# A chunked RWKV-7 recurrence inside a decoder block: the state stacked over the values, 128-row products, batched inverses and a group norm by tokens

## The chip, the cores and the metric

The kernel runs on one core of a Trainium2 chip and is measured in microseconds of device time. Before the change the median of three runs is 2665.36 us (2660.77 to 2671.39). The names of the engines in this text are those of the profile: PE is TensorE (PEld its weight loads), DVE is VectorE, ACT is ScalarE, POOL is GpSimd, SP is SyncE, which issues every DMA of this kernel.

## What is computed

One decoder block on 2048 tokens of width 1024. The input is normed and modulated and multiplied by a combined projection `z = h @ w_in`. Part of `z` feeds a pooling mixer, the rest a RWKV-7 mixer of 8 heads of 64 channels, whose state `S` (64x64 a head) runs through all tokens:

```
def _rwkv7_step(S, inp):
    r, w, k, v, a_vec, b_vec = inp
    sa = jnp.einsum('bhij,bhj->bhi', S, a_vec)
    S = S * w[:, :, None, :] + sa[..., None] * b_vec[:, :, None, :] + v[..., None] * k[:, :, None, :]
    y = jnp.einsum('bhij,bhj->bhi', S, r)
    return S, y
...
    mu = jnp.mean(y, axis=-1, keepdims=True)
    var = jnp.mean(jnp.square(y - mu), axis=-1, keepdims=True)
    yn = ((y - mu) * lax.rsqrt(var + GN_EPS)).reshape(B, T, RWKV_C) * lnx_w + lnx_b
    bonus = jnp.sum(rh * kh * r_k.astype(f32).reshape(N_HEAD, HEAD_N), axis=-1, keepdims=True) * vh
    out = (yn + bonus.reshape(B, T, RWKV_C)) * g
```

Both mixers go through one output projection, the result is added to `x`, and a gated feed-forward layer and a last norm follow.

## The kernel before

The tokens are cut into four batches (`b`) of 512, each batch into 8 chunks (`c`) of 64. There are three stages.

- **Projections.** For each batch `project` makes 18 products of 24 matmuls each (tile `z`, 512 columns). DVE, ACT and POOL make decays, keys and bonuses of them. For every chunk and head the 128x128 Gram products (`gr`, L576) are masked into `gm` and stored in DRAM (`dGM`), beside the decayed queries (`dAR`), keys (`dBH`) and values (`dV`). The 32x32 diagonal blocks are gathered in `N`. `invert` turns them into inverses `W` with 31 steps of a multiply (L284) and an add (L290). For batch 0 that is done here on DVE, for the others later.
- **Chunks.** 32 chunks run one after the other through the state. `chunk` loads its tiles (`cg`, `car`, `cbh`, `cv`), completes the inverse of its 64x64 blocks out of the 32x32 ones (`pq`, L666 and L670, with a copy by ACT behind each), transposes values and keys on PE (`trv`, `trb`), and then walks a chain. `px` is what the Gram block and the state give (L689 from the chunk's own values, L691 from the state `Sb`); ACT copies it to `xx`; `pu` (L699) applies the inverse; ACT copies it into `uv`; `pn` (L704) is the update of the state; two adds by DVE (L707) make the next `Sb`. Beside the chain stands the output `py` (L710 from the state, L713 from `uv`). `Sb` holds two heads block-diagonally, so L691 and L710 take two heads in one matmul. `diagonals(b + 1)` prepares the next batch beside the chunks of this one: it loads `N`, inverts it on POOL and transposes on DVE (L641, L646). After each half of a batch `mixer_norm` makes the group norm with channels in partitions, by products with summing matrices (`pc`, `pv`, `pr`). `out_proj` puts units of 12 projection matmuls of 512 columns (`po`) between the chunks, by a fixed plan.
- **Feed-forward.** Four batches of `gu` and `dn` products of 512 columns.

All products of the chunk stage except `po`, `pc`, `pv` and `pr` are in float32, and each of them stands in the trace as two matmuls (x16 for 8 heads). The order of instructions on every engine is fixed when the program is built: a scheduler that works with its own estimate of times places them, and `issue_after` and `high_priority` bend it. A tile with fewer buffers than users makes the next user wait.

Of the kernel before, what the change touches and what calls it, by code (L numbers as in the profile page):

```python
# [6 lines left out]
F32 = mybir.dt.float32  # L7
F32R = mybir.dt.float32r
AF = mybir.ActivationFunctionType
ALU = mybir.AluOpType  # L10
PSUM = bass.MemoryType.PSUM
# [7 lines left out]
CH = 64  # L19
# [43 lines left out]
def build(tc, io):  # L63
# [39 lines left out]
    dN = [dram.tile([128, 32, 32], F32, name=f"dN{b}") for b in range(NB)]  # L103
    dV = dram.tile([128, 4, 64 + T], F32, name="dV")
# [297 lines left out]
    for b in range(NB):  # L402
# [210 lines left out]
    sp = p1y.tile([128, TB // 2], F32R, name="sp", bufs=1)  # L613
    zero_rows(sp)
    Sb = [p1y.tile([128, 4, 128], F32, name=f"Sb{i}", bufs=1) for i in range(2)]
    G.memset(Sb[0], 0.0)
    G.memset(Sb[1], 0.0)

    for tag, shape, bufs in (("N1", [128, 32, 32], 1), ("W", [128, 32, 32], 1), ("itmp", [128, 256], 1), ("m11", [32, 4, NC, 2, 32], 2)):
        for _ in range(bufs):  # L620
            pe1.tile(shape, F32, tag=tag, name=tag, bufs=bufs)
    MT = pe1.tile([128, 4, NC, 2, 64], F32, name="MT", bufs=1)
    for i in range(2):
        G.memset(MT[64 * i + 32 : 64 * i + 64].rearrange("p a c h t -> p (a c h) t")[:, :, 0:32], 0.0)

    def diagonals(b):
# [3 lines left out]
        W = invert(pe1, N, G) if b else N  # L630
        yield
        o = 64 * (b % 2)
        mu = MT.rearrange("p a c h t -> p (a c h) t")
        m11 = inv[b] = pe1.tile([32, 4, NC, 2, 32], F32, tag="m11", name="m11", bufs=2)
        mm = m11.rearrange("p a c h t -> p (a c h) t")
        for g in range(2):
            us = slice(32 * g, 32 * g + 32)
            for bi in range(2):
# [3 lines left out]
                    mu[o + 32 * bi : o + 32 * bi + 32, us, r].rearrange("p u c -> p c u"),  # L642
# [4 lines left out]
            yield  # L647

    def chunk(b, c, m11, yh, yl):
        o = 64 * (b % 2)  # L650
        mt, lo, hi = MT[o : o + 64], slice(o, o + 32), slice(o + 32, o + 64)
        cc = b * NC + c
        sb, sn = Sb[cc % 2], Sb[(cc + 1) % 2]
        g = p1.tile([128, 8, 128], F32, tag="cg", name="cg", bufs=3)
        Q.dma_start(g, dGM[b][c].rearrange("p x a t -> p (x a) t"))
        a = p1.tile([128, 4, 128], F32, tag="car", name="car")
        Q.dma_start(a, dAR[b][c])
# [4 lines left out]

        qs = p1.tile([128, 8, 32], F32, tag="qs", name="qs")
        ps = ps1.tile([128, 8, 32], F32, tag="gr", name="pq", bufs=1)
        for h in range(8):
            P.matmul(ps[hi, h, :], g[0:32, h, 32:64], m11[:, h // 2, c, h % 2, :], start=True, stop=True)  # L666
# [334 lines left out]
```

## Time and profile before

| | |
|---|---|
| median of the runs | 2665.36 us |
| the profiled execution, its own time | 2662.77 us |
| its span, first to last instruction | 2661.0 us |
| mean granted TensorE clock | 0.976 |
| PE busy | 2531.2 us (95%), 13912 matmuls |
| DVE busy | 1317.1 us (49%) |
| ACT busy | 966.4 us (36%) |
| POOL busy | 457.5 us (17%) |
| DMA | 445.98 MB, mean 168 GB/s |
| chain that ended last | PE 79%, DVE 7%, DMA 6%, ACT 3% |

The busy time of PE counts a matmul from its start to its modelled end, and neighbours overlap. How long a block of matmuls occupies the engine is therefore read from the start of the block to the start of the next one. [...]

### The profile page before, as it was taken

The numbers are of one execution on the slowest core, as the hardware profiler recorded it, in microseconds if no ns is written. First come the engines' busy times: TensorE is split into PE (matmuls) and PEld (weight loads), VectorE is DVE, ScalarE is ACT, GpSimd is POOL, SyncE is SP. The second block draws the span as 40 slices with busy tenths as digits, with TensorE's granted clock in tenths as the row PEclk, the third lists the DMA queues.
The fourth block names the chain that finished last, engine by engine and source line by source line (L and its number), as shares of the span: only waits on it lengthen the run. The fifth ranks groups of instructions, "written<-read, shape, count | busy, mean of one in ns | idle before, by whom it ended". The sixth has DMA issues, their size and how long they took to land.

```text
span 2661.0 us, 35438 instructions
## 1 busy us (share of the span) xinstructions
PE 2531.2 (95%) x13912; PEld 2051.9 (77%) x13912; DVE 1317.1 (49%) x1695; ACT 966.4 (36%) x1490; POOL 457.5 (17%) x516
## 2 busy tenths in 40 slices
PE   5899899997999999799999999999999999999998
PEld 4677677775788878678888888888878888788886
DVE  6668674757567555546334243343343442443322
ACT  3555253443443424423233242332333332333222
POOL 4424333115565300100000020000110000000000
PEclk9899999997999899899999999999999999999998
DMA  8697676876677767655334333234332333333233
GB/s 289 223 314 236 221 268 207 282 258 227 202 246 262 223 218 211 198 185 175 96 101 129 110 127 101 96 95 141 105 127 95 97 104 110 128 101 95 93 111 97
DMA packets 229463, 445.98 MB, mean 168 GB/s; under 512 B 19248, under 2 KB 101424, under 8 KB 229296
## 3 DMA queue, kind: packets, MB, share of 16 engines
q1 hardware_dynamic: 229296, 443.72, 51.2%
q8 instruction: 109, 1.79, 0.3%
q14 instruction: 58, 0.48, 0.1%
HBM read 347.04 MB, written 96.60 MB: 167 GB/s over the span
## 4 chain that ended last, share of the span: by engine, by line
PE 79%; DVE 7%; DMA 6%; ACT 3%; issue 2%; POOL 2%; SPq 0%; DVEq 0%; ACTq 0%; POOLq 0%
PE gu L171 11%; PE gu L170 11%; PE gu L169 11%; PE dn L169 6%; PE dn L170 6%; PE dn L171 6%; PE z L169 3%; PE z L170 3%; PE z L171 3%; PE po L169 2%; PE po L171 1%; PE po L170 1%; DMA wraw<-w_out 1%; PE px L689 1%; PE pu L699 1%
## 5 line engine op out<-in xcount | busy, mean ns | idle before, releaser
L125 DVE TENSOR_TENSOR wlo<-wraw,whi 128x1024 fp32r<-128x1024 f32 (+2 forms) x354 | 400.4, 1131 | 902.7 <-PE gu L170 423.2
L124 ACT CAST whi<-wraw 128x1024 fp32r<-128x1024 f32 (+2 forms) x354 | 337.2, 952 | 780.4 <-DMA wraw<-w_gu 368.9
L169 PE MATMUL gu<-h2h,whi 128*128 128x512 f32 x1408 | 549.3, 390 | 4.5 <-ACT whi L124 4.5
L171 PE MATMUL gu<-h2h,wlo 128*128 128x512 f32 x1408 | 549.7, 390 | 3.6 <-DVE wlo L125 3.6
L170 PE MATMUL gu<-h2l,whi 128*128 128x512 f32 x1408 | 549.0, 390 | 0.0
L241 POOL TENSOR_TENSOR acc<-acc,sq 128x512 f32<-128x512 f32 x76 | 106.2, 1397 | 1451.4 <-ACT sq L237 1150.6
L171 PEld LDWEIGHTS gu<-h2h,wlo 128*128 128x128 f32 x1408 | 264.7, 188 | 61.7 <-DVE wlo L125 7.0
L169 PEld LDWEIGHTS gu<-h2h,whi 128*128 128x128 f32 x1408 | 264.7, 188 | 61.3 <-ACT whi L124 6.4
L170 PEld LDWEIGHTS gu<-h2l,whi 128*128 128x128 f32 x1408 | 264.6, 188 | 54.4
L169 PE MATMUL dn<-ah,whi 128*128 128x512 f32 x704 | 278.2, 395 | 0.0
L171 PE MATMUL dn<-ah,wlo 128*128 128x512 f32 x704 | 278.1, 395 | 0.0
L170 PE MATMUL dn<-al,whi 128*128 128x512 f32 x704 | 278.0, 395 | 0.0
L169 PE MATMUL z<-hh,whi 128*128 128x512 f32 x576 | 233.3, 407 | 11.8 <-ACT whi L124 3.7
L170 PE MATMUL z<-hl,whi 128*128 128x512 f32 x576 | 232.3, 404 | 3.3 <-DVE hl L273 3.3
L171 PE MATMUL z<-hh,wlo 128*128 128x512 f32 x576 | 230.6, 402 | 2.2 <-DVE wlo L125 2.2
L169 PEld LDWEIGHTS dn<-ah,whi 128*128 128x128 f32 x704 | 132.3, 188 | 31.7
L170 PEld LDWEIGHTS dn<-al,whi 128*128 128x128 f32 x704 | 132.3, 188 | 31.7
L171 PEld LDWEIGHTS dn<-ah,wlo 128*128 128x128 f32 x704 | 132.3, 188 | 31.7
L169 PEld LDWEIGHTS z<-hh,whi 128*128 128x128 f32 x576 | 111.2, 193 | 42.4 <-ACT whi L124 3.8
L170 PEld LDWEIGHTS z<-hl,whi 128*128 128x128 f32 x576 | 111.3, 193 | 32.4 <-DVE hl L273 6.0
L171 PEld LDWEIGHTS z<-hh,wlo 128*128 128x128 f32 x576 | 110.7, 192 | 30.9 <-DVE wlo L125 3.3
L898 ACT CAST ah<-th 128x512 fp32r<-128x512 f32 x88 | 54.4, 619 | 199.1 <-DVE th L897 198.7
(329 smaller groups left out, 3372.0 us busy)
## 6 DMA issues: line engine op xcount, KB each, us to landing
wraw<-w_gu SPq DMA_DIRECT2D x176, 512.0 KB, 3.4
wraw<-w_dn SPq DMA_DIRECT2D x64, 512.0 KB, 3.5
whi<-dWI SPq DMA_DIRECT2D x54, 512.0 KB, 4.8
wlo<-dWI SPq DMA_DIRECT2D x54, 512.0 KB, 5.5
dGM<-gm SPq DMA_DIRECT2D x16, 1024.0 KB, 6.0
wraw<-w_out SPq DMA_DIRECT2D x64, 256.0 KB, 3.5
cg<-dGM SPq DMA_DIRECT2D x32, 512.0 KB, 4.7
dX<-xr SPq DMA_DIRECT2D x64, 256.0 KB, 3.5
```

What stands on the lines that cost most here:

```text
L124: S.copy(hi[:, :n, :], raw[:, :n, :])
L125: V.tensor_tensor(lo[:, :n, :], raw[:, :n, :], hi[:, :n, :].bitcast(F32), op=ALU.subtract)
L169: P.matmul(ps, w[0], x[0], start=start, stop=False)
L170: P.matmul(ps, w[0], x[1], start=False, stop=False)
L171: P.matmul(ps, w[1], x[0], start=False, stop=stop)
L241: G.tensor_tensor(acc, acc, sq, op=ALU.add)
L689: box["first"] = P.matmul(px[o : o + 64, h, :], g[64:128, h, 0:64], uv[64:128, h, :], start=h == 0, stop=False, skip_group_check=True)
L699: P.matmul(pu[0:64, h, :], mt[:, h // 2, c, h % 2, :], xx[o : o + 64, h, :], start=True, stop=True)
L898: S.copy(ah[:, f, :], th)
```

## The change

- The state is kept as one tile `SV` for all 8 heads: rows 0 to 63 hold the state (keys by values), rows 64 to 127 the chunk's values. The tile `LL` stacks the queries and the Gram block in the same way. One product over 128 rows a head (`px`, L703) now gives what L689 and L691 gave together. Its lower half, completed by a second product with the whole `cg` tile (L719), is the output, with tokens in partitions. The update `pn` (L712) writes all heads into partitions 0 to 63, and one add (L715) makes the next state. POOL copies the Gram block into `LL` (L681); POOL's product `pss` is one instruction instead of two.
- The completion of the inverses (`pq`, L658 and L662) moves out of `chunk` into `diagonals`: four batches of 16 blocks for every 512 tokens, ahead of the batch that needs them. It loads the off-diagonal Gram blocks (`g21`) in eight DMAs.
- The inversions of batches 1 and 2 move from the chunk stage into the projections, on POOL; that of batch 3 stays.
- The output of a chunk goes to DRAM (`dY`) and comes back by 128 tokens. `mixer_norm` then works with tokens in partitions: two reductions on DVE, a square and a root on ACT, and four transposes on PE (`pt`, L758) back to channels. It runs 16 times on 128 tokens instead of 8 times on 256.

```
-        if b == 0:
-            Q.dma_start(dN[0], invert(pe0, N, V))
-        else:
-            Q.dma_start(dN[b], N)
+        Q.dma_start(dN[b], N if b + 1 == NB else invert(pe0, N, G if b else V))
+        Q.dma_start(dPC[b], pcs[:, b * NC : (b + 1) * NC, :])
...
+    MTs = [pe1.tile([128, 4, NC, 2, 64], F32, name=f"MT{i}", bufs=1) for i in range(2)]
+    LLs = [p1.tile([128, 8, 128], F32, name=f"LL{i}", bufs=1) for i in range(3)]
+    for t in MTs:
+        f = t.rearrange("p a c h t -> p (a c h) t")
+        G.memset(f[64:128], 0.0)
+        G.memset(f[32:64, :, 0:32], 0.0)
...
+        for ct in range(4):
+            ps = ps1.tile([128, 16, 32], F32, tag="gr", name="pq", bufs=1)
+            qs = pe1.tile([128, 16, 32], F32, tag="qs", name="qs", bufs=1)
+            for u in range(16):
+                P.matmul(ps[32:64, u, :], gu[:, 16 * ct + u, :], mm[:, 16 * ct + u, :], start=True, stop=True)
+            S.copy(qs[32:64], ps[32:64])
+            ps = ps1.tile([128, 16, 32], F32, tag="gr", name="pq2", bufs=1)
+            for u in range(16):
+                P.matmul(ps[0:32, u, :], qs[32:64, u, :], mu[32:64, 16 * ct + u, 32:64], start=True, stop=True)
+            S.copy(mu[0:32, 16 * ct : 16 * ct + 16, 32:64], ps[0:32])
+            yield
...
+        for par in range(2):
+            Q.dma_start(lv[0:64, :, par, :], dAR[b][c][64 * par : 64 * par + 64])
+        G.tensor_copy(ll[64:128, :, 0:64], g[64:128, :, 0:64])
...
+                box["first"] = P.matmul(px[:, h, :], ll[:, h, :], sv[:, h, :], start=h == 0, stop=False, skip_group_check=True)
+            xx = p1.tile([128, 8, 64], F32, tag="xx", name="xx")
+            S.copy(xx, px)
+            pu = ps1.tile([128, 8, 64], F32, tag="us", name="pu", bufs=1)
+            for h in range(8):
+                P.matmul(pu[0:64, h, :], mt[:, h // 2, c, h % 2, :], xx[:, h, :], start=True, stop=True)
+            S.copy(sv[0:64], pu[0:64])
+            pn = ps1.tile([128, 8, 64], F32, tag="us", name="pn", bufs=1)
+            for h in range(8):
+                P.matmul(pn[0:64, h, :], bt[:, h, :], sv[:, h, :], start=True, stop=True)
+            if cc + 1 < NB * NC:
+                SV.append(p1.tile([128, 8, 64], F32, tag="SV", name="SV", bufs=3))
+                box["add"] = V.tensor_tensor(
+                    SV[-1][0:64], pn[0:64], pss.rearrange("p a h i -> p (a h) i"), op=ALU.add
                 )
...
         for h in range(8):
+            P.matmul(px[:, h, :], g[:, h, :], sv[:, h, :], start=False, stop=h == 7, skip_group_check=True)
+        yt = p1.tile([128, 512], F32, tag="yt", name="yt", bufs=1)
+        S.copy(yt[64:128], px[64:128].rearrange("p h i -> p (h i)"))
+        Q.dma_start(dY[cc // 2][64 * (cc % 2) : 64 * (cc % 2) + 64], yt[64:128])
...
+        V.tensor_reduce(mean, y8, axis=AXIS_X, op=ALU.add)
...
+        for ct in range(4):
+            P.transpose(pt[:, ct, :], y[:, ct, :], ident)
```

The first place is PE at the start of the chunk stage. Before, two of the small `pq` blocks stand ahead of the first `pu`, and the first chunk's chain goes on at once (L689, L691, L699, L704):

```order
L680 MATMUL trb<-cst,cbh 128x128 x4
L666 MATMUL pq<-m_5074,cg 32x32 x8
L699 MATMUL pu<-xx,MT 64x64 x8
L675 MATMUL trv<-cst,cv 128x128 x4
L670 MATMUL pq_5338<-MT,qs 32x32 x8
L704 MATMUL pn<-uv,bt 64x64 x8
L713 MATMUL py<-cg,uv 64x64 x8
```

Of the changed kernel, the same place, from the third `pq` block on:

```order
L658 MATMUL pq<-m_5304,g_5295 32x32 x16
L703 MATMUL px<-SV,LL_5281 128x64 x8
L693 MATMUL trb<-cst,cbh 128x128 x4
L662 MATMUL pq_5404<-MT_5279,qs 32x32 x9
L708 MATMUL pu<-xx,MT_5279 64x64 x4
L662 MATMUL pq_5404<-MT_5279,qs 32x32 x7
L688 MATMUL trv<-cst,cv 128x128 x4
L708 MATMUL pu<-xx,MT_5279 64x64 x2
L658 MATMUL pq<-m_5304,g_5295 32x32 x16
L662 MATMUL pq_5441<-MT_5279,qs 32x32 x16
L708 MATMUL pu<-xx,MT_5279 64x64 x2
L712 MATMUL pn<-SV,bt 64x64 x8
```

All eight `pq` blocks of the batch, of 16 products each, now stand ahead of the first `pn`, and the last two heads of the first `pu` stand behind the last of them.

The second place is PE in the second chunk, where no projection stands between. Before, from one `pu` to the next `px` with the state:

```order
L699 MATMUL pu<-xx,MT 64x64 x8
L675 MATMUL trv<-cst,cv 128x128 x4
L670 MATMUL pq_5485<-MT,qs 32x32 x8
L704 MATMUL pn<-uv,bt 64x64 x8
L713 MATMUL py<-cg,uv 64x64 x4
L689 MATMUL px<-uv,cg 64x64 x8
L713 MATMUL py<-cg,uv 64x64 x3
L691 MATMUL px<-Sb_5060,car 64x128 x4
```

And of the changed kernel, one whole chunk:

```order
L703 MATMUL px<-SV,LL_5282 128x64 x8
L688 MATMUL trv<-cst,cv 128x128 x4
L708 MATMUL pu<-xx,MT_5279 64x64 x8
L712 MATMUL pn<-SV,bt 64x64 x8
L719 MATMUL px<-SV,cg 128x64 x8
L693 MATMUL trb<-cst,cbh 128x128 x4
```

Between `pu` and `pn` stood a transpose and a `pq` block; now nothing stands there.

The third place is POOL in the projections of the last batch. Before, the splits of the squares (`sqk`) stand in a row, and the split of a bonus (`q`) and the key block (`bh`) follow at once:

```order
L540 MEMSET pp 128x8
L181 TENSOR_TENSOR lo<-sqk,hi 128x512 x4
L544 COPY pcs<-pp 128x8
L181 TENSOR_TENSOR lo<-q,hi 128x512
L564 TENSOR_TENSOR bh<-bk,pp 128x1024
```

Of the changed kernel, the end of the inversion of batch 2 and what stands behind it:

```order
L293 TENSOR_TENSOR W<-W,itmp 128x3x29
L287 TENSOR_TENSOR itmp<-N,W 128x60
L293 TENSOR_TENSOR W<-W,itmp 128x2x30
L287 TENSOR_TENSOR itmp<-N,W 128x31
L293 TENSOR_TENSOR W<-W,itmp 128x31
L543 MEMSET pp 128x8
L184 TENSOR_TENSOR lo<-q,hi 128x512
L547 COPY pcs<-pp 128x8
```

The last 27 instructions of that inversion (L287 and L293 in turn) now stand in a row ahead of this `pp`, and 62 in all between the first `sqk` split and it.

## Rows read from the trace of the kernel before

**Rows 1.** Stages: from:to, length, busy us of the engines, PEclk, DMA share, GB/s

```profile
300.00:600.00 300.00, 287.06 (x1408) 225.31 (x1406) 185.40 (x230) 128.53 (x247) 77.02 (x70) 0.98 0.76 256
...
634.00:672.00 38.00, 25.39 (x203) 20.82 (x203) 22.28 (x19) 10.44 (x20) 19.72 (x35) 0.51 0.78 266
672.00:1103.00 431.00, 418.41 (x4381) 344.38 (x4380) 242.79 (x383) 173.42 (x331) 147.78 (x234) 0.96 0.68 218
1103.00:1149.00 46.00, 31.92 (x114) 22.80 (x114) 40.00 (x54) 23.32 (x38) 10.64 (x7) 0.89 0.80 257
1149.00:2661.00 1512.00, 1494.96 (x6567) 1224.37 (x6566) 589.79 (x684) 475.06 (x586) 66.56 (x47) 0.99 0.35 112
```

**Rows 2.** Timeline of PE where the chunks begin: start, us, instruction, count, idle before

```profile
644.60 0.63 PE L666 MATMUL pq<-m,cg 32*32 32x32 f32 x8 [9.32 <-DVE m L646]
...
650.36 0.63 PE L666 MATMUL pq<-m,cg 32*32 32x32 f32 x8 [3.22 <-DVE m L646]
...
664.35 1.12 PE L704 MATMUL pn<-uv,bt 128*64 128x64 f32 x16
```

**Rows 3.** Timeline of PE in the middle of the chunks, clock 1.00

```profile
999.92 0.69 PE L670 MATMUL pq<-MT,qs 32*32 32x32 f32 x16
1000.54 0.65 PE L675 MATMUL trv<-cst,cv 128*128 128x128 f32 x4
1001.12 0.69 PE L704 MATMUL pn<-uv,bt 128*64 128x64 f32 x16
1001.64 0.64 PE L713 MATMUL py<-cg,uv 128*64 128x64 f32 x16
1002.20 0.69 PE L666 MATMUL pq<-m,cg 32*32 32x32 f32 x16
1002.82 1.14 PE L689 MATMUL px<-uv,cg 64*64 64x64 f32 x16
1003.89 0.66 PE L680 MATMUL trb<-cst,cbh 128*128 128x128 f32 x4
...
1004.95 1.09 PE L691 MATMUL px<-Sb,car 128*64 128x128 f32 x8
1005.96 0.62 PE L670 MATMUL pq<-MT,qs 32*32 32x32 f32 x14
1006.52 1.10 PE L710 MATMUL py<-car,Sb 128*128 128x64 f32 x8
1007.43 0.48 PE L174 MATMUL pc<-yh,sums 128*128 128x512 f32 x1
1007.75 0.39 PE L175 MATMUL pc<-yl,sums 128*128 128x512 f32 x1
1007.98 0.50 PE L374 MATMUL ada<-one,aacc 128*128 128x1 f32 x4
...
1023.39 0.48 PE L754 MATMUL pr<-sp,selT 128*128 128x256 f32 x2
1023.81 0.50 PE L666 MATMUL pq<-m,cg 32*32 32x32 f32 x10
1024.23 0.69 PE L704 MATMUL pn<-uv,bt 128*64 128x64 f32 x16
```

**Rows 4.** Timeline, steps between the products of the chain

```profile
674.12 0.58 ACT L700 COPY uv<-pu 64x512 f32<-64x512 f32 x1 [0.65 <-PE pu L699]
...
676.02 0.88 DVE L707 TENSOR_TENSOR Sb<-pn,pss 64x256 f32<-64x256 f32 x2 [3.83 <-PE pn L704]
...
889.69 1.08 PE L704 MATMUL pn<-uv,bt 128*64 128x64 f32 x16 [0.74 <-ACT uv L700]
```

**Rows 5.** Groups on POOL, 640 to 1103 us: count, busy, mean ns, idle before

```profile
L290 POOL TENSOR_TENSOR W<-W,itmp 128x31 f32<-128x31 f32 (+15 forms) x93 | 56.6, 609 | 7.0
L284 POOL TENSOR_TENSOR itmp<-N,W 128x31 f32<-128x31 f32 (+15 forms) x93 | 51.8, 557 | 19.7 <-DMA N<-dN 12.9
```

**Rows 6.** Timeline of POOL ahead of the chunks

```profile
615.79 3.65 POOL L624 MEMSET MT<- 32x2048 f32 x2 [3.25 <-PE pg L171]
```

More of the change, by code (lines that the diff above doesn't have):

```diff
@@ L10 @@
 ALU = mybir.AluOpType
+AXIS_X = mybir.AxisListType.X
 PSUM = bass.MemoryType.PSUM
@@ L103, in build @@
     dN = [dram.tile([128, 32, 32], F32, name=f"dN{b}") for b in range(NB)]
+    dPC = [dram.tile([128, NC, 4], F32, name=f"dPC{b}") for b in range(NB)]
+    dY = [dram.tile([128, 512], F32, name=f"dY{i}") for i in range(T // 128)]
     dV = dram.tile([128, 4, 64 + T], F32, name="dV")
@@ L612, in build @@
     box = {}
[L613 to L624, printed above, removed]
+    Sb = None
+    for tag, shape in (("N1", [128, 32, 32]), ("W", [128, 32, 32]), ("itmp", [128, 256]), ("m11", [32, 4, NC, 2, 32]), ("g21", [32, 4, NC, 2, 32])):
+        pe1.tile(shape, F32, tag=tag, name=tag, bufs=1)
+    MTs = [pe1.tile([128, 4, NC, 2, 64], F32, name=f"MT{i}", bufs=1) for i in range(2)]
[4 more added lines that the diff above has]
+        G.memset(f[32:64, :, 0:32], 0.0)
+    for t in LLs:
+        G.memset(t[64:128, :, 64:128], 0.0)
     def diagonals(b):
@@ L686, in chunk @@
         with tc.high_priority(offset=100):
-            px = ps1.tile([128, 8, 64], F32, tag="px", name="px")
+            px = ps1.tile([128, 8, 64], F32, tag="px", name="px", bufs=2)
             for h in range(8):
-                box["first"] = P.matmul(px[o : o + 64, h, :], g[64:128, h, 0:64], uv[64:128, h, :], start=h == 0, stop=False, skip_group_check=True)
-            for pr in range(4):
-                P.matmul(
-                    px[o : o + 64, 2 * pr : 2 * pr + 2, :].rearrange("p h i -> p (h i)"), a[:, pr, 0:64], sb[:, pr, :],
-                    start=False, stop=pr == 3, skip_group_check=True,
-                )
@@ L705, in chunk @@
-            for par in range(2):
-                r = slice(64 * par, 64 * par + 64)
-                box["add"] = V.tensor_tensor(sn[r, :, r], pn[r], pss[r], op=ALU.add)
-        py = ps1.tile([128, 4, 64], F32, tag="py", name="py")
-        for pr in range(4):
-            P.matmul(py[:, pr, :], sb[:, pr, :], a[:, pr, 64:128], start=pr == 0, stop=False, skip_group_check=True)
-        for h in range(8):
-            r = slice(64 * (h % 2), 64 * (h % 2) + 64)
-            P.matmul(py[r, h // 2, :], uv[:, h, :], g[:, h, 64:128], start=False, stop=h >= 6, skip_group_check=True)
@@ L762, in build @@
+        into(mh[:, :, cols], ml[:, :, cols], bv)
     rwkv_part, pool_part = {}, {}
@@ L830, in build @@
                 rwkv_part[b] = mh, ml
-            mixer_norm(b, hf, yh, yl, mh, ml)
-            if (b, hf) != (0, 0):
-                out_after(b * NC + 4 * hf + 3)
+            if c % 2 == 1:
+                mixer_norm(b, c // 2, mh, ml)
+            out_after(b * NC + c)
+            if b * NC + c >= 6:
+                with tc.issue_after(box["add"].ins):
+                    for _ in range(3):
+                        next(second, None)
     for _ in second:
```

159 lines of the change are left out of this document (66 added, 93 removed).

## The prediction, made before the run

> **What bounds the kernel now.** I read the stages first. In the feed-forward part PE is busy 1495 of 1512 us at a clock of 0.99, and the change doesn't touch it. Between 300 and 600 us, in the projections, PE is busy 287 of 300 us. From 672 to 1103 us, in the chunks, it is busy 418 of 431 us at 0.96, while DVE has 243 and ACT 173 [rows 1]. So PE sets the time in every stage, and the change counts by what it does to the occupancy of PE, to the waits inside PE's fixed order, and to the clock. Two stretches stand out: 634 to 672 us, where PE is busy 25 of 38 us at 0.51, and the tail from 1103 to 1149 us, 32 of 46 us at 0.89 [rows 1].
>
> Then the timeline of PE. A block's length is the distance to the next start. At the beginning the first product waits 9.3 us and half of it another 3.2 us for DVE's transposes [rows 2]. In the middle the blocks follow each other without idle time [rows 3]. A change of the shape of the array costs time there: a `pq` block of 16 matmuls takes 0.62 us, one of 10 takes 0.42 us, so one matmul takes 0.033 us and about 0.09 us are left for the change to the next shape. From one 128x128 block to another there is no such rest.
>
> **The change part by part, in PE's occupancy.** Without the 0.09 us where the next shape differs, from [rows 3]:
> - `pn` alternates between the two halves of the output partitions and takes 0.52 us for 16 matmuls. `px` L689 writes one half only and takes 1.07 us. The new `pn` writes one half only, so I price it like L689: 0.55 us more, 32 times, is +17.6 us. Its other bound is that it stays at 0.52.
> - `px` took 1.07 (L689) and 1.01 us (L691), 1.90 without two changes of shape. The new one is 16 matmuls with 128x128 weights and 64 columns. L710 is 8 of that kind in 0.91 us, so it takes 1.82: -2.6 us over 32 chunks.
> - `py` took 0.91 (L710) and 0.56 us (L713), 1.38 without one change. The new one is again 1.82: +14.1 us.
> - `pu`, the transposes and `pq` keep their number of matmuls: 0.
> - The norm: per half `pc` is twice 0.32 and 0.23, `pr` four at 0.21, and `pv` eight of 256 columns, which I estimate at half of `pc`'s 0.23. That is 2.9 us, 8 times 23.2. The new transposes `pt` are blocks of four like `trv`, 0.49 without the change, 16 times 7.8: -15.4 us.
> - Changes of shape on PE, counted along the order from the first chunk product to the first gate product: 387 before, 197 after. 190 times 0.09 is -17.1 us.
>
> The sum is -3.4 us. The occupancy hardly moves.
>
> [...]
>
> **What it does to the waits.** From `pu` to `pn` ACT's copy takes 0.58 us [rows 4]; with the handing over on both sides I price the step without cover at 0.75 us, close to the one wait of this kind in the trace, 0.74 us at 889 us [rows 4]. Before, `trv` and a `pq` block stand in that gap. In the new order 8 of the 32 `pn` have nothing between them and `pu`, 7 have one block of four transposes (0.55 us), the others more. 8 times 0.75 and 7 times 0.2 is 7.4 us. Between `px` and `pu` five chunks have only a transpose: 5 times 0.17 is 0.9 us. Together +8.3 us; between nothing and 0.75 us at all 32 `pn`, 24 us. The third step, `pn` to the add (0.88 us as two instructions, [rows 4], one of twice the columns now) to the next `px`, is covered by 1.82 us of `py` and a transpose; it costs nothing unless DVE comes over 1.2 us late.
>
> **Where the chunks begin.** DVE's transposes still end the wait at 650 us. The eight `pq` blocks of 32 matmuls, 1.15 us each at full clock (0.62 plus 16 times 0.033), now all run before the first `pn`; the stretch runs at 0.51. Before, two chunks' worth of them, 2.5 us, did so. The difference, 6.7 us, is work taken from later chunks, but at half clock it takes as much again; some of it fits in the 3.2 us wait, so I take +3.5 us. POOL has more to clear first: two memsets of 2048 columns take 3.65 us [rows 6]; the new ones clear four times 2048 columns more at the same rate, 7.3 us, and parts of three `LL` tiles. Some 9 us of it are new and stand before the copies that `px` needs. Half of that hides under the transposes, as the chunk's first `px` stands behind the third `pq` block; I take +2 us, bounds 0 and 9.
>
> **What leaves the chunk stage.** An inversion is 31 of each of two instructions: (56.6 + 51.8) / 3 = 36 us of POOL [rows 5]. Two of them go to the projections, where POOL is busy 77 of 300 us [rows 1], so 72 us more leave it half idle. Queued behind them there are the splits that PE's `pk` and `pb` products need, and the memset of `pp`, which `ar` and `gr` need; PE has projections of 24 matmuls to fill in. I take 0, with bounds of 0 and 27 instructions of 0.58 us, 16 us. In the chunks POOL did not hold PE up, so nothing is won there. The state's own extra traffic (`LL` in two DMAs, `g21`, `dY` out and in) meets DMA engines at a share of 0.68 [rows 1]; the loads are issued chunks ahead, and I take 0. ACT's and DVE's sums change little, and neither bounds.
>
> The tail keeps its order on PE, eight units of `po` and then the gate products, with the same loads and splits behind it: 0.
>
> In all: -3.4 + 8.3 + 3.5 + 2 = +10.4 us on 2662.8 us of the profiled execution, 2673 us. That execution lies 2.6 us below the median of the runs, so 2673 to 2676 us; I say 2674 us. A measurement of this kernel tells a difference from about 0.5%, 13 us, so this is "no change", on the slow side.
>
> **Rivals.**
> 1. The chain takes the place of PE's work as the bound. `px`, `pu` and `pn` now wait for each other with less between them than before, where L689, both `pq` blocks and the transposes needed no state. For it speaks the 0.74 us wait at 889 us. If ACT is late by that much more, being busy with other copies, at the 15 thinly covered `pn`, that is 11 us more; and if the first four chunks, which have no projections between, stay at 1.2 GHz as PE did until 672 us, half of the 28 us of work of four chunks (`px` and `py` 1.82 us each, `pu` and `pn` 1.07, two transposes 0.6: 7 us) is added once more, 14 us. 2674 + 25 is 2699 us. Against it: the two units of `po` that each later chunk has, 24 matmuls at `pc`'s 0.23 us or 5.5 us [rows 3]. It decides from about 0.4 us of idle time a chunk more than I count.
> 2. POOL's inversions hold up the projections. If each of the two stands for its 16 us ahead of what PE needs next and half is not covered by other products, PE idles 16 us: 2690 us. Against it: POOL's idle half.
> 3. The clock. Of 672 to 1103 us a mean of 0.96 means 8% of the time, 34 us, at 1.2 GHz, and 634 to 672 us is there almost whole. In the latter PE was busy 25 of 38 us with products of 32 and 64 rows and stayed low. If products over 128 rows bring the clock up, half of the 34 us and half of the 38 are worked at full speed and give back half their length, 18 us; with half as many copies by ACT behind `pq` blocks of twice the size, some 7 us of waits as well, an estimate of 0.2 us for each of the chunks: 2649 us. Against it: from 672 us on the same small products stand in nearly every chunk, at a mean of 0.96.
> 4. PE's new products are cheaper than I price. If `pn` keeps 0.52 us, 17.6 us go: 2656 us. If a change of shape costs a whole pass through the array, 0.2 us (a `pq` block's 0.69 us from start to last end, less 15 times 0.033), the 190 changes bring another 20 us: 2654 us. Both together make 2636 us. Against the second: one matmul's worth of `pq` plus 0.09 us fits blocks of 10 and of 16 alike.
>
> **How the numbers follow.** Forecast 0.37, on its own 2658 to 2678 us. Rival 1 has 0.26, rival 2 has 0.10, rival 3 has 0.18, rival 4 has 0.09. Rivals 1 and 2 are slower by over 0.5%, above 2679 us: 0.36. Rival 3, and rival 4 with both its parts, lie below 2652 us: 0.27. The forecast is the rest, 0.37. The range for 8 in 10 takes in rivals 1 and 3 and leaves out their ends: 2644 to 2706 us.
>
> **What would show it.** In the profile after: `pn` blocks of 16 at about 1.07 us and both kinds of `px` blocks at 1.8 us; idle time of some 0.7 us before `pn`, released by ACT, in about eight chunks; a chunk stage as long as now to within 15 us; no wait of PE on POOL's splits beyond a few us. A `pn` block near 0.5 us, a clock of 0.98 or more over the chunks, or more than 20 us of idle time of PE on ACT or DVE in them would prove me wrong.

## The result, and the profile after

The changed kernel takes 2778.99 us (median of 4 runs, 2776.34 to 2779.47) against 2663.07 us for the kernel before: a ratio of 1.0436, 95% interval 1.0396 to 1.0477. The forecast was no change, 2674 us. The profiled execution has a span of 2774.5 us, 113.5 us more than before. Its stages, from the windows view of the changed kernel (same columns as [rows 1]: stretch, length, busy us of PE, PEld, DVE, ACT and POOL with their instruction counts, granted clock, DMA share, GB/s):

```profile
300.00:600.00 300.00, 246.08 (x1184) 189.50 (x1183) 174.35 (x204) 113.89 (x219) 144.44 (x192) 0.91 0.65 218
...
688.90:771.70 82.80, 74.71 (x613) 68.69 (x613) 19.80 (x27) 24.87 (x42) 13.68 (x19) 0.56 0.63 178
771.70:1212.30 440.60, 403.53 (x3380) 349.86 (x3380) 230.84 (x397) 146.07 (x261) 95.51 (x121) 0.90 0.72 215
1212.30:1260.50 48.20, 33.01 (x123) 23.68 (x123) 40.46 (x68) 20.89 (x35) 11.06 (x7) 0.79 0.81 263
1260.50:2774.50 1514.00, 1494.12 (x6568) 1223.06 (x6568) 591.68 (x684) 474.98 (x585) 68.27 (x47) 1.00 0.35 113
```

PE was busy 287 of the 300 us between 300 and 600 us [rows 1]; now it is 246, at 0.91. The chunks run at 0.56 in their first four and 0.90 in the others. The tail and the feed-forward part are as long as before, to 3 us.

To say where 113 us went, I split each stage of PE's timeline three ways. "Idle" is the time from the modelled end of one matmul to the start of the next. "Lost" is half of the time at half clock less half of the idle time in it, an estimate of what the same products would have saved at full clock. "Work" is the rest. Half and full clock are granted clocks of 0.50 and 1.00, the only two values in the clock records of the two profiled executions, so a mean between them tells how much of a stretch had either. The traces give these shares and no frequency; the 1.2 GHz of the prediction and the expectations is the half clock. In the changed kernel products of 512 columns start 0.427 us apart at half clock (581.21 to 583.77 us), 1.2 columns a ns, and 0.233 us apart at full clock (585.05 to 594.85 us), 2.2 a ns; a `pn` takes 1.90 us and 1.07. That is less than two to one, so "lost" is on the high side.

| stage (us) | before: length, idle, lost, work | after: length, idle, lost, work | difference |
|---|---|---|---|
| start to last `gr` | 633.2, 58.8, 12.9, 561.5 | 671.3, 97.4, 15.0, 559.0 | +38.1 |
| to first `pq` | 11.4, 9.5, 0.7, 1.3 | 17.6, 12.9, 1.0, 3.8 | +6.2 |
| to chunk 4's update | 61.8, 5.1, 11.7, 44.9 | 82.7, 8.0, 32.9, 41.8 | +20.9 |
| to the last update | 395.9, 10.6, 15.1, 370.2 | 440.6, 37.1, 42.1, 361.4 | +44.7 |
| tail, to first `gu` | 46.0, 14.2, 4.6, 27.3 | 48.2, 15.2, 6.1, 26.9 | +2.2 |
| feed-forward | 1512.7, 8.3, 7.9, 1496.5 | 1514.0, 11.1, 6.1, 1496.7 | +1.3 |

Chunks are counted from 0. So there are three main losses: 38 us of waiting in the projections, 21 us of half clock in the first four chunks, and 45 us in the others, of waits (26.5) and half clock (27.0), against 8.8 us of work saved.

**The projections.** PE's timeline of the changed kernel, where the inversion of batch 2 runs:

```profile
542.86 0.50 PE L172 MATMUL z<-hh,whi 128*128 128x512 f32 x1 [0.50 <-DMA whi<-dWI]
...
551.35 0.80 PE L550 MATMUL pn<-nkp,selT 128*128 128x512 f32 x1 [6.30 <-DVE nkp L194]
580.62 0.80 PE L174 MATMUL z<-hh,wlo 128*128 128x512 f32 x1 [28.47 <-DMA wlo<-dWI]
```

A projection begins at 542.86 us with the rounded part of its weights (`whi`), and its third product waits 28.47 us for the remainder, `wlo`. Why `wlo` is late stands in the timeline of SP, which issues one DMA after the other:

```profile
538.43 0.37 SPq L137 DMA_DIRECT2D whi<-dWI  x1
558.39 0.37 SPq L568 DMA_DIRECT2D dBH<-bh  x1
573.60 0.32 SPq L600 DMA_DIRECT2D dN<-W  x1
577.06 0.32 SPq L137 DMA_DIRECT2D wlo<-dWI  x1
```

Between `whi` and `wlo` two stores stand in the queue. What each waited for, from the view of waits, SP alone, 520 to 600 us (waiting line, what for, total, times, longest):

```profile
SPq L568 <- POOL bh L567: 19.6, 1, 19.6
SPq L600 <- POOL W L293: 14.8, 1, 14.8
```

And the two instructions on POOL:

```profile
556.46 1.90 POOL L567 TENSOR_TENSOR bh<-bk,pp 128x1024 f32<-128x1024 f32 x1
...
573.32 0.25 POOL L293 TENSOR_TENSOR W<-W,itmp 128x31 f32<-128x31 f32 x1
```

POOL makes the key block `bh` only at 556.46 us, in the middle of the inversion, and ends the inversion at 573.57. SP stands behind both, and with it a weight load that has nothing to do with either.

**The chunks.** In the first four, at half clock, a whole step of the chain:

```profile
734.14 1.97 PE L712 MATMUL pn<-SV,bt 128*64 128x64 f32 x16 [0.72 <-ACT SV L709]
736.04 3.68 PE L719 MATMUL px<-SV,cg 128*128 128x64 f32 x16
```

At full clock, from a later chunk, the prices of the new products:

```profile
1062.66 1.15 PE L712 MATMUL pn<-SV,bt 128*64 128x64 f32 x16
1063.73 2.00 PE L719 MATMUL px<-SV,cg 128*128 128x64 f32 x16
1065.66 0.56 PE L662 MATMUL pq<-MT,qs 32*32 32x32 f32 x12
```

From start to start `pn` takes 1.07 us and the second `px` 1.93. One of the longer stops, PE and then ACT:

```profile
859.12 1.15 PE L708 MATMUL pu<-xx,MT 128*64 128x64 f32 x16
...
864.89 1.97 PE L712 MATMUL pn<-SV,bt 128*64 128x64 f32 x16 [3.53 <-ACT SV L709]
```

```profile
863.74 0.62 ACT L127 CAST whi<-wraw 128x512 fp32r<-128x512 f32 x1 [5.64 <-DMA wraw<-w_out]
864.27 0.57 ACT L709 COPY SV<-pu 64x512 f32<-64x512 f32 x1
```

`pu` was done by 860.3 us, but the copy that `pn` needs stood on ACT behind a cast that waited 5.64 us for a weight load. PE went back to half clock 3.0 us into that stop, and the block of `pn` then took 1.9 us and not 1.07. Such waits of ACT's cast are 131.6 us in 40 times over the chunks (690 to 1215 us), and were 53.2 us in 28 times (645 to 1103 us):

```profile
ACT whi L127 <- DMA wraw<-w_out: 131.6, 40, 7.5
```

```profile
ACT whi L124 <- DMA wraw<-w_out: 53.2, 28, 6.2
```

### The profile page after: what moved, and what is told of

Its sections match the earlier page's. It is cut to its first block, busy times and chain, and to the rows that moved or that the text cites. A ratio compares the mean times of both kernels' runs of the same rounds, so it can differ in the third digit from the quotient of the medians.

```text
span 2774.5 us, 34549 instructions
## 1 busy us (share of the span) xinstructions
PE 2569.7 (93%) x13336; PEld 2104.7 (76%) x13336; DVE 1326.6 (48%) x1742; ACT 953.6 (34%) x1441; POOL 477.6 (17%) x520
## 4 chain that ended last, share of the span: by engine, by line
PE 73%; DMA 10%; DVE 8%; POOL 4%; ACT 2%; issue 2%; SPq 1%; DVEq 0%; ACTq 0%; POOLq 0%
PE gu L174 11%; PE gu L173 11%; PE gu L172 11%; PE dn L172 6%; PE dn L173 6%; PE dn L174 6%; PE z L174 3%; PE z L172 3%; PE z L173 3%; PE px L703 2%; PE px L719 2%; PE po L172 1%; DMA adaw<-ada 1%; DMA wraw<-w_out 1%; PE po L173 1%
## 5 line engine op out<-in xcount | busy, mean ns | idle before, releaser
L172 PEld LDWEIGHTS gu<-h2h,whi 128*128 128x128 f32 x1408 | 264.8, 188 | 60.9 <-ACT whi L127 6.2
L174 PE MATMUL z<-hh,wlo 128*128 128x512 f32 x576 | 233.2, 406 | 33.1 <-DMA wlo<-dWI 29.4
```

What stands on the lines that cost most here:

```text
L172: P.matmul(ps, w[0], x[0], start=start, stop=False)
L174: P.matmul(ps, w[1], x[0], start=False, stop=stop)
```

## The experiments

Unless it is said otherwise each is one edit of the changed kernel. Ratios are to the kernel before on the same chip, with 95% intervals; the changed kernel's is 1.0436 (1.0396 to 1.0477). Total times of two kernels tell about 12 us apart. The kernel before itself has medians of 2663 to 2678 us beside the different runs, so a gain is given in the medians and, where it matters, against each run's own kernel before (the changed kernel is 116 us above its own). Smaller things are read from the stages of one profiled execution each. The two runs that add products to the first four chunks leave the later ones alone; from chunk 4 on they idle 30.1 and 34.5 us and lose 33.9 and 49.3 us to the clock, where the changed kernel has 37.1 and 42.1. Differences of some 10 us in these figures therefore tell nothing.

**The inversions back in the chunks.**

```
-        Q.dma_start(dN[b], N if b + 1 == NB else invert(pe0, N, G if b else V))
+        Q.dma_start(dN[b], invert(pe0, N, V) if b == 0 else N)
-        W = invert(pe1, N, G) if b + 1 == NB else N
+        W = invert(pe1, N, G) if b else N
```

> The changed kernel with the inversions of batches 1 and 2 back in the chunk stage (still on POOL). Theory A: in the projections SP's queue stands still behind the store of POOL's key block and the store of the inverse (34 us together), the weight load behind them comes late and PE waits 28.5 us and falls to half clock. Then the projections end at 630 to 636 us instead of 671, and the time falls by 34 to 42 us, to 2737 to 2745 us. Rival: the projections are longer for another reason (new stores, the order of the loads): less than 10 us come back, 2769 us or more. A third outcome, that POOL's inversions in the chunks hold up the copies of the Gram block or the products for the state, would give back less than 30 us with the projections at 634 us.

Measured 2750.89 us, 1.0274 (1.0212 to 1.0337). The projections end at 638.1 us and PE's idle time in them is 60.7 us, as before the change. The gain is 28 us in the medians and 38 us against its own kernel before, so the total does not decide between theory A and the third outcome. In the profiled execution the chunks with the tail are 10 us longer (581.6 for 571.6), which is the third outcome if it is more than the spread. From the windows view of this run, the projections and the chunks with the tail:

```profile
0.00:638.10 638.10, 563.05 (x2650) 441.94 (x2650) 420.37 (x558) 284.79 (x516) 205.77 (x191) 0.97 0.75 250
...
655.80:1237.40 581.60, 517.57 (x4113) 446.36 (x4113) 295.59 (x492) 191.86 (x337) 191.87 (x271) 0.83 0.70 209
```

**The kernel before, with the inversions alone moved.** The same two places the other way round.

> The kernel before with one part of the change alone: the inversions of batches 1 and 2 run in the projections on POOL, nothing else is changed. Theory A: the same stop of SP's queue appears in the last batch, the projections end at 665 to 675 us instead of 634, and the time is 30 to 42 us above the kernel before, 2693 to 2705 us. Rival: the stop needs the rest of the change (its order of loads); then the time stays within 10 us of the kernel before.

Measured 2716.59 us, 1.0152 (1.0101 to 1.0203), 44 us above its base, a little more than theory A said. The projections end at 679.6 us (633.2 in the kernel before), and SP's waits are those of the changed kernel:

```profile
SPq L565 <- POOL bh L564: 18.6, 1, 18.6
SPq L597 <- POOL W L290: 14.7, 1, 14.7
```

```profile
582.77 0.80 PE L171 MATMUL z<-hh,wlo 128*128 128x512 f32 x1 [27.90 <-DMA wlo<-dWI]
```

Undone on one side and done alone on the other, this part costs 33 to 46 us in the projections. That cause is shown.

**The norm reads older tokens, and the weights' wait is taken away, apart and together.** The first run has the first edit alone, the second the other. The third has both, and leaves out the loads of the weights too.

```
-        Q.dma_start(y.rearrange("p a t -> p (a t)"), dY[4 * b + q])
+        Q.dma_start(y.rearrange("p a t -> p (a t)"), dY[max(4 * b + q - 1, 0)])
...
+        src = C("sm").rearrange("p (a b) -> p a b", b=128) if n == 4 else raw[:, :n, :]
-        S.copy(hi[:, :n, :], raw[:, :n, :])
+        S.copy(hi[:, :n, :], src)
```

> The changed kernel, except that the norm loads the output of the 128 tokens before its own (the first its own), which landed long ago: the traffic is the same, the wait for the round trip through DRAM is gone. It norms the wrong tokens. Theory B: what is queued on DVE and ACT behind a late load (the mean behind the load of y, the weight cast behind its load) holds the copies of the chain, and the clock falls after each such stop. Then DVE's wait for y (41 us) goes, PE's idle time from the first pq to the first gate product falls from 60 to 40 to 50 us and the loss by the clock there from 81 to 65 to 75 us: 15 to 35 us less, 2744 to 2764 us. Rival C, the chain's own hops (pu, copy, pn) are the idle time: less than 6 us, 2773 us or more.

> The changed kernel, except that the cast and the split of the output projection's weights read a resident constant tile and not the loaded one; the loads are issued as before and read by nobody. The output projection is computed with wrong weights. Theory B: ACT's 132 us of waits for these loads go, with them the longest stops of the chain (3.5 us at 861, 2.1 at 950, 3.5 at 997, 4.5 at 1167), and the half-clock stretches behind them: 20 to 45 us less, 2734 to 2759 us, PE idle from the first pq to the first gate product 30 to 45 us. Rival C: less than 8 us, 2771 us or more, since the waits of ACT lie beside the chain.

> The changed kernel without the 64 loads of the output projection's weights (cast and split read a constant tile) and with the norm reading the output of 128 tokens before: neither ACT's cast nor DVE's mean can wait for a load now. Its output projection and norm are wrong. Taking either wait away alone gave 12 us and nothing. Theory B, in the form that each of the two waits hides the other: PE idle from the first pq to the first gate product falls from 60 to under 40 us, the clock's loss there from 81 to under 60, the time by 30 to 55 us, 2724 to 2749 us. Rival C (the chain waits for its own hops and for PE's own order): less than 15 us, 2764 us or more.

Measured 2766.39 us, 1.0349 (1.0292 to 1.0406); 2783.11 us, 1.0401 (1.0347 to 1.0456); and 2752.84 us, 1.0312 (1.0275 to 1.0348). Idle from the first `pq` to the first `gu` is 57.6, 60.2 and 49.4 us (60.3 in the changed kernel), lost to the clock 82.3, 98.5 and 74.2 (81.1). Alone neither does what theory B said. But the edits did not take away all that they aimed at. By the view of waits, from the first `pq` to the last update, DVE's `mean` still waits 29.6 us in 6 times for the load of `y` in the first run and 48.2 us in 11 in the third (41.5 in 10 in the changed kernel): older tokens did not make that load early. In the second, DVE's split still waited 60.9 us for the load in the cast's place. Both together give 26 us in the medians (32 against its own kernel before), less than expected or at its lower end, and the clock hardly recovers. For the cast theory B is tested here; for `y` it is not.

**SP relieved, and two buffers for the norm.** Of the first run (beside a store of the queries that fits) and of the second:

```
-        for par in range(2):
-            Q.dma_start(lv[0:64, :, par, :], dAR[b][c][64 * par : 64 * par + 64])
+        Q.dma_start(ll[0:64], dAR[b][c].rearrange("p a h t -> p (a h) t"))
...
-            xr = box["q"].tile([128, TB], F32, tag="xr", name="xr", bufs=4)
+            xr = box["q"].tile([128, TB], F32, tag="xr", name="xr", bufs=8)
```

```
-            return box["q"].tile([128, 4, 128], F32, tag=name, name=name, bufs=1)
+            return box["q"].tile([128, 4, 128], F32, tag=name, name=name, bufs=2)
```

> The changed kernel with SP relieved: the queries are stored so that one DMA loads a chunk's LL (32 fewer in the chunks, 16 more in the projections), and the tile xr has 8 buffers and not 4, so that SP does not stand behind the stores of the output projection (57 us of waits). Theory E: SP's queue, with about 120 more DMAs in the chunk stage than before, is what makes the loads late that ACT and DVE wait for: 15 to 40 us less, 2739 to 2764 us, and PE idle from the first pq to the first gate product 35 to 50 us. Rival: the loads come as late, since the buffers that they fill come free late: within 6 us of the changed kernel.

> The changed kernel with two buffers for each of the norm's four tiles, so that its loads can go out while the norm before is still at work. Theory F in the form that the late loads of the norm are what ACT and DVE stand behind: 12 to 35 us less, 2744 to 2767 us. Rival: the loads are late because of their place in SP's queue, or the norm's own steps are what holds the copies: within 8 us of the changed kernel.

Measured 2770.66 us, 1.0383 (1.0347 to 1.042), idle 60.9 us; and 2780.28 us, 1.0397 (1.0365 to 1.0428), idle 56.2 us. SP's load and the norm's buffers are not the cause by themselves.

**No norm at all, after and before.** The body of `mixer_norm` goes but for its last line:

```
-        into(mh[:, :, cols], ml[:, :, cols], bv)
+        into(mh[:, :, cols], ml[:, :, cols], C("sm").rearrange("p (a t) -> p a t", t=128))
```

> The changed kernel without its group norm: no loads of the chunk's output, bonus and gate, no statistics, no transposes; the projection gets a constant tile, cast and split as before. Theory F: the new norm, 16 times with one buffer for each of its tiles, puts steps into ACT's and DVE's queues that wait for loads and for each other, and the copies of the chain stand behind them. Then, from chunk 4 to the end of the chunks, PE idle (37 us) falls to 10 to 20, the loss by the clock (42 us) to 15 to 28; with 9 us of PE work less the time falls by 45 to 70 us, 2709 to 2734 us. Rival: the norm is one user of late loads among others: its own work and under 15 us of waits go, 2755 to 2770 us.

> The kernel before without its group norm, in the same way (a constant tile goes to the projection). It is the measure for the run above: what the old norm cost. Its PE work is 23 us; its waits in the chunks are few (10.6 us idle from chunk 4 on, 15 us lost by the clock). Theory F: 20 to 32 us less than before, 2633 to 2645 us, and the new norm thus costs 25 to 40 us more than the old one. Rival: as much or more comes off here as in the run above, 45 us or more.

Measured 2775.91 us, 1.0396 (1.0327 to 1.0466), against 2656.7 us, 0.9945 (0.992 to 0.997). From chunk 4 on idle falls from 37.1 to 25.2 us, but the clock loses 52.3 us instead of 42.1. Theory F fails; the 10 us more by the clock are within the spread. In the kernel before, the norm's absence saves 28.8 us of PE work there, and the loss by the clock doubles, from 15.1 to 30.3 us. With the old norm, products of 256 and 512 columns (`pc`, `pv`, `pr`) left the chunks. That this is why the clock lost more is a hint from one execution: the run with the inversions alone moved, which has all these products, lost 23.3 us there.

**The cast on POOL, and the norm and the weights' loads both taken away.** The first run has this edit, the second neither the norm nor the weights' loads.

```
-        S.copy(hi[:, :n, :], raw[:, :n, :])
+        (G.tensor_copy if n == 4 else S.copy)(hi[:, :n, :], raw[:, :n, :])
```

> The changed kernel with the cast of the output projection's weights on POOL and not on ACT; nothing is left out. If ACT's queue is the place where the chain is held (131.6 us of its waits in the chunks are those of this cast for its load), PE's waits for ACT from chunk 4 on (31 us) are halved and the time falls by 15 to 45 us, 2734 to 2764 us. Rival: POOL, which copies the Gram block and makes the product for the state, stands behind the loads in ACT's place, and the time is within 10 us of the changed kernel or longer.

> The changed kernel without the group norm and without the 64 loads of the output projection's weights (both replaced by a constant tile), so that of the work that stands in ACT's queue between the copies of the chain nearly nothing waits for a load. Theory G, that the two hold the copies in turn, each hiding the other: from chunk 4 on PE's idle time falls from 37 to below 20 us and the clock's loss from 42 to below 30, the time is 2700 to 2735 us. Rival C (the chain's own hops, and the clock falls without any late load because the short products of a chunk stand together): idle above 22, loss above 40 us, 2750 us or more.

The cast on POOL: 2785.56 us, 1.0432 (1.041 to 1.0453). PE's idle time from chunk 4 on falls from 37.1 to 28.1 us, the tail gets 7 us longer, the time stays: the rival. Without the norm and the weights' loads: 2751.22 us, 1.0295 (1.0269 to 1.0322), idle 21.9 us from chunk 4 on, lost 43.2. So theory G fails, and rival C comes out but for its idle time, which lies just below the 22 us that it named. Not every late load was gone, though. DVE still waits 68.1 us in 17 times over the chunks for weights of the modulation (`adaw`; 45.9 us in the changed kernel), and the longest stop of PE, 7.27 us, stands behind such a wait, DVE first, then PE:

```profile
917.40 0.48 DVE L375 SCALAR_TENSOR_TENSOR aacc<-adaw,cact,aacc 128x256 f32<-128x256 f32 x1 [11.98 <-DMA adaw<-ada]
...
919.06 0.68 DVE L717 TENSOR_TENSOR SV<-pn,pss 64x512 f32<-64x512 f32 x1
```

```profile
919.79 3.67 PE L705 MATMUL px<-SV,LL 128*128 128x64 f32 x16 [7.27 <-DVE SV L717]
```

No run takes these loads away. But the clock is lost without late loads as well. PE's timeline of that run shows how:

```profile
828.66 0.39 PE L176 MATMUL po<-mph,wlo 128*128 128x512 f32 x1
828.89 0.60 PE L690 MATMUL trv<-cst,cv 128*128 128x128 f32 x4
...
832.68 1.19 PE L664 MATMUL pq<-MT,qs 32*32 32x32 f32 x32
...
834.54 0.62 PE L710 MATMUL pu<-xx,MT 128*64 128x64 f32 x4
835.88 1.97 PE L714 MATMUL pn<-SV,bt 128*64 128x64 f32 x16 [0.72 <-ACT SV L711]
837.78 3.68 PE L721 MATMUL px<-SV,cg 128*128 128x64 f32 x16
...
842.10 3.51 PE L705 MATMUL px<-SV,LL 128*128 128x64 f32 x16
...
846.23 0.77 PE L174 MATMUL po<-mph,whi 128*128 128x512 f32 x1
...
852.13 1.15 PE L710 MATMUL pu<-xx,MT 128*64 128x64 f32 x16
```

```profile
826.00:834.00 8.00, 7.87 (x96) 6.44 (x95) 1.35 (x2) 2.46 (x5) 0.61 (x1) 0.89 0.33 86
834.00:852.00 18.00, 17.20 (x80) 15.36 (x78) 2.94 (x6) 4.02 (x7) 1.84 (x2) 0.53 0.51 143
852.00:856.00 4.00, 3.28 (x42) 2.94 (x41) 1.83 (x4) 1.16 (x2) 0.00 (x0) 1.00 0.46 131
```

Full clock had come back at 827.8 us, in a block of `po`. From 828.9 us on PE has only short products, and no wait above 0.13 us; at 834.7 us the clock falls. `pn` then takes 1.90 us and the second `px` 3.47 from start to start, where the next chunk, at full clock, has 1.08 and 1.83. Twelve `po` matmuls come at 846.23, and full clock is back at 851.7 us. Of the ten half-clock stretches of this run from chunk 4 on, five begin like this one, with no longer wait of PE in the 10 us before.

**Dense and short products in the first four chunks, dense ones held back, dense ones everywhere.** Behind `pu`:

```
+            if cc < 4:
+                with tc.issue_after(solved.ins):
+                    for _ in range(4):
+                        P.matmul(dz, bd, selT.rearrange("p a b -> p (a b)"), start=True, stop=True)
```

> The changed kernel with four added products of 512 columns in each of the first four chunks, between pu and pn, into a tile that nobody reads: 16 products, 3.7 us at full clock. Theory D: PE stays at 1.2 GHz from 677 to 762 us, in the four chunks that have no projections, because its short products with a 0.7 us wait in every chunk do not bring the clock up; with dense products in the wait it comes up by 725 us, the half-clock stretch shrinks from 85 to under 55 us, and the time falls by 8 to 18 us although work was added: 2761 to 2771 us. Rival: the clock does not depend on them; then the added work shows, less the waits that it fills: 2781 to 2785 us.

> As the run with dense products in the first four chunks, but with four float32 products of 64 columns in their place (0.9 us as well). Theory D, that the kind of product counts and not the filled wait: the half-clock stretch at the beginning of the chunks stays at 70 us or more (73 in the changed kernel, 38.6 with the products of 512 columns), and the four chunks take 84 to 92 us. Rival, that the 0.7 us wait in every chunk is what keeps the clock low: the stretch falls below 55 us.

Dense: 2773.44 us, 1.0382 (1.0338 to 1.0426). Short: 2784.21 us, 1.0413 (1.0378 to 1.0448). The stretch from the first `pq` to chunk 4's update, of the dense and of the short run:

```profile
689.10:762.60 73.50, 64.54 (x629) 56.88 (x629) 16.95 (x25) 24.63 (x42) 13.90 (x19) 0.74 0.67 192
```

```profile
685.60:768.30 82.70, 73.01 (x645) 67.37 (x645) 18.79 (x28) 24.66 (x42) 12.95 (x19) 0.64 0.63 178
```

With 16 added products of 512 columns the stretch is 9 us shorter than in the changed kernel (82.7), 38.6 us of it are at half clock, and full clock first comes at 724.3 us, as theory D said. With 16 float32 products of 64 columns in the same gaps the stretch is as long as without; its half-clock time, 59.6 us, is neither the 70 of theory D nor the 55 of the rival, and the same stretch, not edited, has 57 to 85 us in other runs. What the kind of product does is read from the timelines. The dense run, where a chunk then takes 8 us and not 13:

```profile
720.04 2.08 PE L713 MATMUL dz<-selT,sums 128*128 128x512 f32 x4
722.05 1.97 PE L717 MATMUL pn<-SV,bt 128*64 128x64 f32 x16
723.95 2.17 PE L724 MATMUL px<-SV,cg 128*128 128x64 f32 x16
```

The short run, whose first added block takes about as long:

```profile
717.64 1.97 PE L713 MATMUL dz<-cst 128*128 128x64 f32 x8
...
731.81 1.10 PE L713 MATMUL dz<-cst 128*128 128x64 f32 x8
732.85 1.15 PE L717 MATMUL pn<-SV,bt 128*64 128x64 f32 x16
```

Here full clock comes at 731.6 us, with short products alone, and the next chunk takes 8 us too. After two waits of 1.3 to 1.4 us for ACT both runs fall back, the dense one from 748.2 to 751.7 us, the short one from 748.6 to 762.3. And in the changed kernel, where four transposes of the norm stand in chunk 3 in place of the wait:

```profile
759.77 1.12 PE L758 MATMUL pt<-cst,y 128*128 128x128 f32 x4
760.82 1.68 PE L712 MATMUL pn<-SV,bt 128*64 128x64 f32 x16
762.42 2.00 PE L719 MATMUL px<-SV,cg 128*128 128x64 f32 x16
...
766.41 0.48 PE L172 MATMUL po<-mph,whi 128*128 128x512 f32 x1
```

Full clock comes at 762.0 us, before the first `po`. So with the wait filled full clock came at 724.3 us with wide products and at 731.6 us with short ones, in one execution of each run. That the filled wait or the kind of product decides is not shown.

The held projections:

```
-                next(last_pool_mixer)
+                with tc.issue_after(box["first"].ins):
+                    next(last_pool_mixer)
```

> The changed kernel, but the four pool projections of the last batch (96 matmuls of 512 columns, 22.4 us) are held back behind the first px of chunks 0 to 3, so that these chunks have dense products between their steps. Theory D: the clock comes up in the first chunk, some 20 us of half clock and 3 us of waits are saved: 2750 to 2764 us. Rival: the work is only moved, the wait ahead of the first pq (6.1 us) and that ahead of the last pm grow or stay, and the clock does as before: 2772 to 2786 us.

Measured 2787.62 us, 1.0455 (1.0421 to 1.0488): a miss. The projections end 8.4 us earlier, half clock up to chunk 4's update falls from 73 to 37 us, and all of it goes again, since the held projections leave their place empty and the later chunks are 11 us longer.

The dense products in every chunk (`if cc < 4` goes; they write into the bank of `trv`), after and before:

> The changed kernel with four added products of 512 columns behind pu in every chunk, not in the first four alone: 128 products, 30 us of PE work at full clock, into a tile that nobody reads. Theory D: from chunk 4 on, too, PE loses the clock (42 us there) because its chunks are made of short products with waits between; with the dense ones the loss from chunk 4 on falls below 22 us and PE's idle time by 5 to 10 us, so that the added work costs little: 2760 to 2785 us. Rival: the half-clock stretches follow the waits alone, which the added products do not shorten; the loss stays at 38 us or more and the work is paid: 2790 to 2805 us.

> The kernel before with the same four products of 512 columns behind pu in every chunk. It loses only 15 us by the clock from chunk 4 on and waits little, so by every theory the 30 us of work are paid here to the most part: 2680 to 2695 us. If theory D holds, the difference between this run and its base is at least 10 us larger than that between the changed kernel with and without these products.

Measured 2807.58 us, 1.0499 (1.0467 to 1.0531), and 2724.2 us, 1.0184 (1.0153 to 1.0214). From chunk 4 on the changed kernel still loses 52.3 us by the clock and idles 40.4: theory D in the form "any dense products will do" fails there. The work costs 29 us in the changed kernel (13 against its own kernel before) and 46 in the one before; that difference is the one that theory D named, but since the loss from chunk 4 on did not fall it proves little.

**Together.** Inversions in the chunks, dense products in the first four, one DMA for `LL`, two buffers in the norm; then with dense products in every chunk.

> Three of the edits together on the changed kernel: the inversions of batches 1 and 2 in the chunks, dense products in the first four chunks, one DMA for LL and two buffers for the norm's tiles. If the parts add up: 28 us (inversions), 6 (dense products), 5 to 8 (LL), 0 to 30 (norm): 2707 to 2740 us. If the waits replace each other: 2740 to 2752 us. No theory has it below the kernel before.

> The best version so far (inversions in the chunks, one DMA for LL, two buffers in the norm) with the dense products in every chunk and not in the first four alone. Theory D: 2715 to 2735 us; rival, the added work is paid: 2745 to 2760 us.

Measured 2734.37 us, 1.0227 (1.0179 to 1.0275), the best of the changed forms, and 2754.48 us, 1.0304 (1.0261 to 1.0346), where the added work is paid, as the rival said. About half of the loss comes back; none beats the kernel before.

## Why the prediction was wrong

The forecast left out 105 us. Two of its terms were put at 0 and cost tens of microseconds, the inversions in the projections and the waits behind late steps in the chunks, and its sum has no term for the clock beyond the chunks' start.

- **PE's occupancy.** Right in kind. At full clock a `pn` block takes 1.075 us at the median (I said 1.07), the two `px` blocks 1.76 and 1.84 us (1.82). The sum of the chunk stage and tail fell by 12.3 us (442.4 to 430.1, the work column) and not by 3.4. The runs without a norm point at the norm's term, which I had at -15.4 us: without the old norm this work falls by 29.4 us (442.4 to 413.0), without the new one by 0.3 (430.1 to 429.8). What the order of the other products changes with it is in these figures too.
- **"I take 0" for the inversions on POOL.** This step failed first. I asked which of PE's products need a split by POOL, and these account for some 10 us at most (4.3 us in three waits for `pk`, 6.3 for `pn` of the projections, which waited for DVE). I never followed the stores: `dBH` waits for POOL's `bh`, `dN` for the last `W`, and both stand in SP's queue ahead of PE's weights. My rival on POOL, 16 us, had the place and not this path; it costs 33 to 46 us.
- **The chain's handovers, +8.3 us.** These came as counted: eight bare waits of 0.72 us ahead of `pn` and two shorter ones, 6.2 us together, where 7.4 were forecast. But idle time rose by 30.4 us in the chunks and tail. Most of the rest are stops of 1 to 4.5 us in which PE waits for a copy by ACT or an add by DVE. Without the norm and the weights' loads 21.9 of the 37.1 us from chunk 4 on stay, so these two explain some 15 us of them.
- **"The loads are issued chunks ahead, and I take 0."** Wrong for ACT: its casts wait 131.6 us and not 53.2. Taking the candidates away one by one gave 13 us or less in the medians (22 or less against each run's own kernel before), two together 26 us (32), norm and weights together 28 us (36). None of these edits alone brings the loss back; the share of each source stays open, the more so as the waits for `y` outlived two of the edits and those for `adaw` all of them.
- **Where the chunks begin, +3.5 and +2 us.** It is +27 us (6.2 to the first `pq`, 20.9 to chunk 4's update), of which 21 us are half clock.
- **The clock.** The sum has no term for it beyond the start, and it carries most of the chunks' loss: 81.1 us for 31.4. My rival 3 had the sign wrong; rival 1 named the first four chunks with 14 us as a mere extra, and the loss there rose by 21.2. What I left out is in [rows 3]: `po`, `pc` and `pr` of 256 and 512 columns stood between the short products all along. In the changed kernel the short ones stand together, and the norm has no wide ones left. Each of the 12 half-clock stretches from chunk 4 on begins while PE has short products or waits, or right behind them, and ten of them end when, or after, `po` products have come again. That the missing wide products are the cause is argued and not shown: four of them put into every chunk left the loss from chunk 4 on at 52.3 us. Nor does the clock go with PE's busy time alone: PE was busy 74.7 of 82.8 us in the first four chunks, at half clock for 73 of them, and 246 of the 300 us from 300 to 600 us, in the projections, at a mean of 0.91.
- **The chances.** Rivals 1 and 2 were priced as alternatives, 25 and 16 us. Both happened at once, each two to three times as large. That took the time past the upper end of the range.

## What to carry to other kernels

When instructions move to another stage, follow each of their results to the queue that stores it and read what stands behind that store; here two stores held SP's queue for 34 us, and PE waited 28.5 us for the weights behind them. Count not only how much time a product takes but what waits and what clock its block will see: here 12.3 us of work were saved from the first `pq` to the first gate product, while idle time rose by 30.4 us and the loss to the clock by 49.7. A saving of PE work below the waits that it uncovers is no saving. And look whether an edit that is to take a wait away did so: here the load of `y` stayed late in both runs that aimed at it.

## What the runs showed of the hardware that was not expected

PE stayed at half clock (0.50 from 676.7 to 762.0 us) through the first three chunks, the last two of them with a single wait of 0.72 us in each 13.2 us. With four products of 512 columns in that wait full clock came at 724.3 us; with four of 64 columns, as long, it came at 731.6 us; with neither, at 762.0, in the first chunk without the wait. In other runs that add nothing to these chunks it came between 729 and 773 us. And in the run without the norm and the weights' loads the clock fell at 834.7 us, when PE had had only short products since 828.9 and no wait above 0.13 us.
